# A second engine multiplies the x tiles of a split-precision projection: GpSimd writes the products to scratch, VectorE subtracts

## The chip, the cores and the metric

The kernel runs on one core of a Trainium2 chip. The time is the device time of one execution in microseconds; of the kernel before there are three runs, 1316.72 to 1316.91 us, with a median of 1316.73. Engines are named as in the profile: PE (TensorE), DVE (VectorE), ACT (ScalarE), POOL (GpSimd), SP (SyncE, which issues the loads).

## What is computed

One inference step of a hybrid decoder layer for 256 prompt rows and 8 sample rows (N = 264 columns in the kernel, D = 2048). Only the head of it bears on this case:

```python
xn = rms_norm(x, g_mix)
z = xn @ w_in                       # 2048 x 3584, split among three mixers
...                                 
gates = jax.nn.sigmoid(xn @ w_gate + b_gate)
x = x + (g_a * y_pool + g_b * y_lru + g_c * y_conf) @ w_out
hid = jnp.square(jax.nn.relu(rms_norm(x, g_mlp) @ w_up))
x = x + hid @ w_down
```

Everything is float32, and the result has to be good to nearly that, so the kernel multiplies in three parts (below).

## The kernel before, in words

**Layout.** Channels lie on the 128 partitions, the 264 rows of x along the free dimension. x is 16 tiles of 128x264 (k = 0 to 15). Weights stream from HBM in chunks of two such k-tiles by 512 columns, through six raw slots (`raw`).

**Split products.** TensorE multiplies a rounded format (fp32r). Each operand is therefore kept as a rounded part and a rest: for weights `whi` and `wlo`, for x the two halves of the tile `A`. A product is three matmuls of 128x264: whi by x-high, wlo by x-high, whi by x-low (`mm`, `mm3`, line 255).

**Where each part is made.** For weights, `split` lets ACT cast a chunk to `whi` (L238) and DVE subtract to get `wlo` (L239); for the first four k-tiles, which come in four small head loads with their x tiles, `cast_head` (L248) and `rest_head` (L252) do the same in halves of 256 columns. For x, the tile times the norm's factor of its channel (`gm`, one column for each k, 128 factors) is rounded by `x_high`: on DVE for k = 0 and 1 (L367), on ACT for the others (L369). `x_low` then calls `rest_of` (L171): three DVE instructions of 128x88, each computing x times factor minus the rounded tile and rounding the rest. The normalisation itself is applied later, to the products.

**Order.** The schedule is written out by hand: each engine runs its instructions in the order in which the code issues them, and waits on semaphores. The opening issues for k = 0 to 3: cast of the first half weight, x_high, cast of the second half, x_low, the two weight rests. Then x tiles 4 and 5 and the split of chunk 2; then, in the chunk loop for i = 0 to 4, x tiles 2i+6 and 2i+7 and the split of chunk i+3. PE's matmuls of chunk i follow. For the first four chunks (`by_operand`) they go tile by tile: four with whi and x-high, four with whi and x-low, four with wlo and x-high. From chunk 4 on the three of one output block follow one another.

**Buffers.** `G` is scratch of 24 rows of 128x264. Rows 0 to 7 and 20 to 23 take the squares of x for the norm (L382, L387), later users come after that. POOL has three small memsets at the start, and its next work, the series in `softplus` (L418 and on), at 43 us.

Of the kernel before, what the change touches and what calls it, by code (L numbers as in the profile page):

```python
# [12 lines left out]
ALU = mybir.AluOpType  # L13
# [103 lines left out]
def hybrid_step(ctx: ExitStack, tc: tile.TileContext, first, par_in, st_in, wall, y_out, st_out):  # L117
    nc = tc.nc
# [4 lines left out]
    def f(ap):  # L123
        return ap.bitcast(F32)
# [13 lines left out]
    G = cpool.tile([P, 24, N], F32, name="G")  # L138
# [12 lines left out]
    def both(t, place, row, rows):  # L151
        out = []
        for low in (0, rows * ROW + GAP):
            at = SKEW + row * ROW + place * OCT + low
            out.append(bass.AP(tensor=t.tensor, offset=t[:, at:].offset,
                               ap=[list(t.ap[0]), [HOP, N // (STRETCH * OCT)], [STEP, STRETCH], [1, OCT]]))
        return tuple(out)

    def in_a(k):
        return both(a_all, k // 2, k % 2 + k // 8 * 2, 4)  # L160
# [4 lines left out]
    def v(t):  # L165
        return t.rearrange("p (a b c) -> p a b c", b=STRETCH, c=OCT)

    def rest_of(to, x, g):
        for a in range(N // (STRETCH * OCT)):
            hi, lo, t = to[0][:, a], to[1][:, a], v(x)[:, a]  # L170
            nc.vector.scalar_tensor_tensor(lo, t, g, f(hi), op0=ALU.mult, op1=ALU.subtract)  # L171
# [38 lines left out]
    gm = head[0]  # L210
# [4 lines left out]
    def head_x(k):  # L215
        return head[k // 2][:, head_at(k):head_at(k) + N]
# [145 lines left out]
    def x_of(k):  # L362
        return head_x(k) if k < 4 else X[:, k, :]

    def x_high(k):
        if k < 2:
            nc.vector.tensor_scalar(in_a(k)[0], v(x_of(k)), gm[:, k:k + 1], None, op0=ALU.mult)  # L367
        else:
            nc.scalar.activation(in_a(k)[0], v(x_of(k)), AF.Copy, scale=gm[:, k:k + 1])  # L369

    def x_low(k):
        rest_of(in_a(k), x_of(k), gm[:, k:k + 1])

    def x_tile(k):
        x_high(k)
        x_low(k)
# [588 lines left out]
    for k in range(4):  # L965
        cast_head(k, 0)
        x_high(k)
        cast_head(k, 1)
        x_low(k)
        for h in range(2):  # L970
            rest_head(k, h)
# [220 lines left out]
```

## Time and profile before

| | |
|---|---|
| median of three runs | 1316.73 us (1316.72 to 1316.91) |
| the profiled execution | 1317.18 us |
| its span, first to last instruction | 1315.4 us |
| mean granted TensorE clock | 0.997 |
| first x tile and factors landed | 4.2 us |
| DVE between 4.24 and 25.70 us | 21.39 us busy of 21.46 |
| POOL's first work after the memsets | 43.16 us |

The profiled execution lies 0.45 us above the median, and its span 1.8 us below its own time; the difference is start and end around the instructions. A row of a view by time gives start, length, engine, line, operation, the tile written and the tiles read with their shapes, the count where rows were merged, and in brackets the idle time before it with what ended it. A group's row gives the number, the busy time in us and the mean in ns.

### The profile page before, as it was taken

To read this page: it belongs to the slowest core of one execution; us is meant where nothing else is said; L and a number is where in the kernel's file an instruction comes from. 1 tells how busy PE (TensorE), PEld (TensorE's weight loads), DVE (VectorE), ACT (ScalarE), POOL (GpSimd) and SP (SyncE) were. 2 spreads that over 40 slices of the span, in tenths; PEclk is the share of its full clock that TensorE was granted. 3 is DMA by queue.
4 is the path that set the end of the run, shared out by engine and by line. 5 is a ranking of instruction groups with operands and counts; after the bars stand their busy time and mean duration, and the time that the engine had idled before them with its cause. 6 is when DMAs were issued, how large, how long until landed. Compare 5 with 4: busy or idle time off the path is not lost.

```text
span 1315.4 us, 26547 instructions
## 1 busy us (share of the span) xinstructions
PE 1304.1 (99%) x11421; PEld 1301.1 (99%) x11421; DVE 842.0 (64%) x1130; ACT 720.6 (55%) x1035; POOL 99.5 (8%) x125
## 2 busy tenths in 40 slices
PE   9999999999999999999999999999999999999997
PEld 8999999999999999999999999999999999999996
DVE  8786888776777668666655455655455645465554
ACT  7667677667675645455544334543344533354544
POOL 0230020110102014021000000000000000000012
PEclk9999999999999999999999999999999999999998
DMA  9656556555565555555555555555555555555552
GB/s 331 207 177 234 174 200 213 193 193 193 192 225 193 193 193 191 194 192 193 193 192 192 193 194 193 193 194 192 193 194 194 195 195 194 195 195 195 192 197 76
DMA packets 40822, 257.48 MB, mean 196 GB/s; under 512 B 4481, under 2 KB 6785, under 8 KB 11777
## 3 DMA queue, kind: packets, MB, share of 16 engines
q1 hardware_dynamic: 40272, 255.19, 56.4%
q8 instruction: 89, 1.46, 0.4%
q10 hardware_dynamic: 432, 0.61, 0.1%
q14 instruction: 29, 0.23, 0.1%
HBM read 252.57 MB, written 3.21 MB: 194 GB/s over the span
## 4 chain that ended last, share of the span: by engine, by line
PE 98%; DVE 1%; DMA 0%; issue 0%; DVEq 0%; ACT 0%
PE acc L255 98%; DVE A L171 1%; DMA tmp<-first_dram 0%; DVE y L1078 0%; DVE wlo L239 0%; DVE wlo L252 0%; DVE A L367 0%; DVE acc L1069 0%; DVEq L1169 0%; DVE G L1068 0%; DVE acc L1067 0%; PE acc L1055 0%; PE acc L334 0%; ACT rstd L1062 0%; DVE G L894 0%
## 5 line engine op out<-in xcount | busy, mean ns | idle before, releaser
L239 DVE TENSOR_TENSOR wlo<-raw,whi 128x1024 fp32r<-128x1024 f32 (+1 forms) x478 | 585.2, 1227 | 450.3 <-ACT whi L238 444.5
L238 ACT CAST whi<-raw 128x1024 fp32r<-128x1024 f32 (+1 forms) x478 | 494.5, 1037 | 535.8 <-PE acc L255 490.4
L255 PE MATMUL acc<-A,whi 128*128 128x264 f32 x3968 | 678.0, 275 | 0.3 <-DVE A L367 0.3
L255 PEld LDWEIGHTS acc<-A,whi 128*128 128x128 f32 x3968 | 596.6, 187 | 1.3 <-ACT whi L248 0.8
L255 PE MATMUL acc<-A,wlo 128*128 128x264 f32 x1984 | 541.3, 275 | 0.6 <-DVE wlo L239 0.4
L255 PEld LDWEIGHTS acc<-A,wlo 128*128 128x128 f32 x1984 | 370.2, 187 | 1.4 <-DVE wlo L239 1.4
L255 PE MATMUL acc<-xn,whi 128*128 128x264 f32 x2048 | 349.9, 275 | 0.0
L255 PEld LDWEIGHTS acc<-xn,whi 128*128 128x128 f32 x2048 | 308.5, 188 | 0.0
L255 PE MATMUL acc<-xn,wlo 128*128 128x264 f32 x1024 | 281.0, 274 | 0.0
L255 PEld LDWEIGHTS acc<-xn,wlo 128*128 128x128 f32 x1024 | 192.0, 188 | 0.0
L255 PE MATMUL acc<-Q,whi 128*128 128x264 f32 x776 | 144.9, 275 | 0.0
L255 PE MATMUL acc<-LH,whi 128*128 128x264 f32 x768 | 143.7, 276 | 0.0
L255 PEld LDWEIGHTS acc<-Q,whi 128*128 128x128 f32 x776 | 122.4, 188 | 0.0
L255 PEld LDWEIGHTS acc<-LH,whi 128*128 128x128 f32 x768 | 121.2, 188 | 0.0
L255 PE MATMUL acc<-Q,wlo 128*128 128x264 f32 x388 | 106.6, 275 | 0.0
L255 PE MATMUL acc<-LH,wlo 128*128 128x264 f32 x384 | 105.7, 275 | 0.0
L864 POOL TENSOR_TENSOR G<-G 128x264 f32<-128x264 f32 x28 | 25.7, 919 | 754.0 <-ACT G L862 753.0
L255 PEld LDWEIGHTS acc<-Q,wlo 128*128 128x128 f32 x388 | 72.8, 188 | 0.0
L255 PEld LDWEIGHTS acc<-LH,wlo 128*128 128x128 f32 x384 | 72.0, 188 | 0.0
L648 ACT ACTIVATE G<-tmp,par 128x256 f32<-128x256 f32 x120 | 54.3, 499 | 2.5 <-DVE G L651 1.7
L651 DVE TENSOR_TENSOR G<-G 128x1024 f32<-128x1024 f32 x30 | 38.2, 1274 | 0.0
L897 DVE TENSOR_TENSOR X<-X,acc 128x264 f32<-128x264 f32 x79 | 28.7, 423 | 6.5 <-PE acc L255 6.5
(173 smaller groups left out, 522.1 us busy)
## 6 DMA issues: line engine op xcount, KB each, us to landing
raw<-wall_dram SPq DMA_DIRECT2D x226, 1024.0 KB, 4.8
raw<-wall_dram SPq DMA_DIRECT2D x12, 512.0 KB, 5.1
raw<-first_dram SPq DMA_DIRECT2D x6, 512.0 KB, 7.9
X<-first_dram SPq DMA_DIRECT2D x6, 264.0 KB, 7.8
raw<-wall_dram SPq DMA_DIRECT2D x5, 256.0 KB, 2.9
tmp<-first_dram SPq DMA_DIRECT2D x3, 388.0 KB, 4.5
y_dram<-y SPq DMA_DIRECT2D x3, 264.0 KB, 2.2
tmp<-st_dram SPq DMA_DIRECT2D x4, 188.0 KB, 5.1
```

What stands on the lines that cost most here:

```text
L171: nc.vector.scalar_tensor_tensor(lo, t, g, f(hi), op0=ALU.mult, op1=ALU.subtract)
L238: nc.scalar.copy(h, r)
L239: nc.vector.tensor_tensor(lo, r, f(h), op=ALU.subtract)
L255: nc.tensor.matmul(ps[:, :N], w[k == 1], x[k == 2], start=start, stop=stop)
L648: nc.scalar.activation(dst[:, ct, :TP], vext[:, ct, k:k + TP], AF.Copy, scale=par[:, w:w + 1])
L651: nc.vector.tensor_tensor(VC[:, :, :TP], VC[:, :, :TP], src[:, :, :TP], op=ALU.add)
L864: nc.gpsimd.tensor_tensor(sq2, sq2, t, op=ALU.add)
L897: nc.vector.tensor_tensor(X[:, m, :], X[:, m, :], ps[:, :N], op=ALU.add)
```

## The change

GpSimd now multiplies each x tile by its factors, in float32, and leaves the product in a scratch row, `G[:, 8 + k % 12, :]`. `x_low` is one subtraction on DVE over the whole tile: scratch row minus rounded tile, rounded. And the rounded tile for k = 1 is made by GpSimd instead of DVE. ACT's rounded tiles for k from 2 on stay as they were.

```diff
     def x_high(k):
         if k < 2:
-            nc.vector.tensor_scalar(in_a(k)[0], v(x_of(k)), gm[:, k:k + 1], None, op0=ALU.mult)
+            eng = nc.gpsimd if k else nc.vector
+            eng.tensor_scalar(in_a(k)[0], v(x_of(k)), gm[:, k:k + 1], None, op0=ALU.mult)
         else:
             nc.scalar.activation(in_a(k)[0], v(x_of(k)), AF.Copy, scale=gm[:, k:k + 1])
+        t = G[:, 8 + k % 12, :]
+        nc.gpsimd.tensor_scalar(t, x_of(k), gm[:, k:k + 1], None, op0=ALU.mult)
 
     def x_low(k):
-        rest_of(in_a(k), x_of(k), gm[:, k:k + 1])
+        hi, lo = in_a(k)
+        nc.vector.tensor_tensor(lo, v(G[:, 8 + k % 12, :]), f(hi), op=ALU.subtract)
```

How it stands on DVE in the opening, from the first x tile on (with - what stood there before, with + what stands there now; `tmp_70` and `tmp_71` are the two tiles of the head loads with x, factors and weights for k = 0, 1 and k = 2, 3):

```order
-L367 TENSOR_SCALAR A<-tmp_70 128x3x11x8
-L171 SCALAR_TENSOR_TENSOR A<-tmp_70,A 128x11x8 x3
+L368 TENSOR_SCALAR A<-tmp_70 128x3x11x8
+L376 TENSOR_TENSOR A<-G,A 128x3x11x8
 L252 TENSOR_TENSOR wlo<-tmp_70,whi 128x256 x2
-L367 TENSOR_SCALAR A<-tmp_70 128x3x11x8
-L171 SCALAR_TENSOR_TENSOR A<-tmp_70,A 128x11x8 x3
+L376 TENSOR_TENSOR A<-G,A 128x3x11x8
 L252 TENSOR_TENSOR wlo<-tmp_70,whi 128x256 x2
-L171 SCALAR_TENSOR_TENSOR A<-tmp_71,tmp_70,A 128x11x8 x3
+L376 TENSOR_TENSOR A<-G,A 128x3x11x8
```

Three pieces became one instruction, which reads a row of `G` and so waits for POOL; the second TENSOR_SCALAR is gone from DVE. The weight rests between them stay where they were.

POOL's list at the same place, before (its three memsets, then the start of `softplus`):

```order
L358 MEMSET qtmp 128x4x15
L418 ISA
L418 TENSOR_TENSOR G<-G 128x8
L419 TENSOR_TENSOR G<-G 128x8
L421 MEMSET G 128x8
```

and now:

```order
L358 MEMSET qtmp 128x4x15
L372 ISA
L372 TENSOR_SCALAR G<-tmp_70 128x264
L368 TENSOR_SCALAR A<-tmp_70 128x3x11x8
L372 TENSOR_SCALAR G<-tmp_70 128x264
L372 TENSOR_SCALAR G<-tmp_71,tmp_70 128x264 x2
L372 TENSOR_SCALAR G<-X,tmp_70 128x264 x12
L422 TENSOR_TENSOR G<-G 128x8
```

Seventeen instructions came in ahead of `softplus`: the product for k = 0, the rounded tile for k = 1 and then its product, and the products of the other tiles, each as soon as its x has landed (and, from k = 12 on, as soon as DVE has read the scratch row that it reuses). The ISA row, which stands ahead of POOL's first operation on tensors, moved from `softplus` to the first product.

## The prediction

> **What bounds the kernel now.** I read the page first: the busy shares and the chain that ended last.
>
> ```profile
> PE 1304.1 (99%) x11421; PEld 1301.1 (99%) x11421; DVE 842.0 (64%) x1130; ACT 720.6 (55%) x1035; POOL 99.5 (8%) x125
> PE 98%; DVE 1%; DMA 0%; issue 0%; DVEq 0%; ACT 0%
> ```
>
> TensorE (PE) is busy for 99% of the span and holds 98% of the chain. The change touches the opening alone, where x is split into a rounded tile and its rest, so the next view is the chain of waits of the first 80 us.
>
> ```profile
> 19.62 1.15 DVE wlo L239
> 20.77 0.04 issue
> 20.82 22.01 PE acc L255 x191
> ...
> 42.95 37.06 PE acc L255 x326
> ```
>
> Up to 20.82 us the chain runs through DVE (and the first landing); from there it is PE without a break. So the opening is worth what PE loses before 20.82 us, and no more. That is counted from the busy time by window, for the matmuls of L255 (columns: window, its length, PE busy and count, weight loads, clock, DMA share, GB/s), and named in the waits of the weight loads between 4 and 21 us.
>
> ```profile
> 4.87:20.82 15.95, 15.37 (x122) 14.24 (x122) 1.00 1.03 397
> 20.82:42.83 22.01, 22.01 (x192) 21.96 (x193) 1.00 0.75 260
> ...
> PEld acc L255 <- DVE wlo L239: 1.2, 3, 0.6
> PEld acc L255 <- ACT whi L248: 0.8, 1, 0.8
> PEld acc L255 <- DVE A L171: 0.4, 2, 0.2
> ```
>
> After 20.82 us a matmul costs 22.01 / 192 = 0.1146 us. The 122 of the opening would take 13.98 us at that rate, and took 15.95: **1.97 us are lost**, all but the first 0.8 us of ACT wait (which lies before the first matmul) on DVE. That is the most that the change can give: 0.15% of 1317 us. My bound between a change and no change is 0.2% (2.63 us), about what a measurement of this kernel can tell from no change. So a gain that counts is out of reach from the start; the question is how much of the 1.97 us comes back, or whether something is paid on top.
>
> DVE has no hole in that stretch (columns as above, with DVE, ACT, POOL behind the weight loads):
>
> ```profile
> 4.24:25.70 21.46, 20.56 (x165) 19.15 (x164) 21.39 (x68) 19.09 (x36) 0.00 (x0) 1.00 1.01 384
> ```
>
> 21.39 of 21.46 us are DVE work and POOL does nothing. PE's last wait on it, for the second weight rest `wlo` of chunk 5, ends at 20.82 us; each microsecond that DVE reaches this instruction sooner or later goes to PE, until another wait takes over.
>
> **What goes from DVE.** In order of time, one x tile of DVE's list, and further on the same subtraction as the new one (128x264, two SBUF operands, rounded output):
>
> ```profile
> 6.10 0.48 DVE L367 TENSOR_SCALAR A<-tmp 128x264 fp32r<-128x264 f32 x1
> 6.62 0.75 DVE L171 SCALAR_TENSOR_TENSOR A<-tmp,A 128x88 fp32r<-128x88 f32 x3
> 7.29 0.76 DVE L252 TENSOR_TENSOR wlo<-tmp,whi 128x256 fp32r<-128x256 f32 x2
> ...
> 98.75 1.80 DVE L517 TENSOR_TENSOR L<-G,L 128x264 fp32r<-128x264 f32 x5
> 100.46 1.22 DVE L239 TENSOR_TENSOR wlo<-raw,whi 128x1024 fp32r<-128x1024 f32 x1
> ```
>
> Instructions overlap a little, so I count from start to start. Three L171 pieces: 7.29 - 6.62 = 0.67 us. One L517: (100.46 - 98.75) / 5 = 0.34 us. Each x tile saves 0.33 us. The second rounded tile (L367) goes to POOL and saves 6.62 - 6.10 = 0.52 us. Up to the `wlo` of chunk 5 DVE handles 12 x tiles: 12 x 0.33 + 0.52 = **4.5 us less** of its own work.
>
> **What POOL adds.** Seventeen instructions of 128x264: 16 products into scratch and one rounded tile. POOL idles, but not for free, as the one place shows where POOL and DVE both work on SBUF in small pieces:
>
> ```profile
> 83.35 1.65 DVE L488 TENSOR_TENSOR G<-G,tmp 128x1024 f32<-128x1024 f32 x1
> 84.92 1.23 DVE L239 TENSOR_TENSOR wlo<-raw,whi 128x1024 fp32r<-128x1024 f32 x1
> 86.08 1.25 DVE L488 TENSOR_TENSOR G<-G,tmp 128x1024 f32<-128x1024 f32 x1
> 87.25 1.21 DVE L239 TENSOR_TENSOR wlo<-raw,whi 128x1024 fp32r<-128x1024 f32 x1
> ...
> 83.87 1.20 POOL L505 COPY st<-tmp 128x24 f32<-128x24 f32 x1
> 85.01 1.24 POOL L750 COPY st<-qtmp 128x60 f32<-128x60 f32 x1
> ```
>
> A COPY of 24 elements takes 1.20 us: it stands until DVE's L488 is over (83.35 + 1.65 = 85.00) and ends 0.07 us later. The COPY of 60 ends at 86.25, 0.10 us after DVE's L239 (86.15). So the two engines take turns, one whole instruction each, where DVE reads two SBUF operands. And DVE waits in its turn: behind the COPY of 60 its instruction takes 1.25 instead of 1.21 us. How it looks with a POOL instruction of the new length, but with two operands:
>
> ```profile
> 252.31 1.77 DVE L651 TENSOR_TENSOR G<-G 128x1024 f32<-128x1024 f32 x1
> ...
> 249.83 4.85 POOL L817 TENSOR_TENSOR tmp<-G 128x264 f32<-128x264 f32 x4 [69.04 <-DVE G L814]
> ```
>
> DVE takes 1.77 us for what takes 1.21 alone: 0.56 us. The new subtractions and all the `wlo` instructions read two operands from SBUF, so nearly every POOL instruction falls between two of them.
>
> **The price of one POOL instruction to DVE is the unknown of this sum.** The trace has no TENSOR_SCALAR of POOL longer than 8 elements.
>
> ```profile
> 46.71 1.22 DVE L464 TENSOR_TENSOR tmp<-G,rstd 128x1024 f32<-128x1024 f32 x1
> 46.94 1.05 POOL L424 TENSOR_SCALAR G<-G 128x8 f32<-128x8 f32 x1
> 48.07 0.20 POOL L423 TENSOR_TENSOR G<-G 128x8 f32<-128x8 f32 x1
> ```
>
> It ends at 47.99, 0.06 us after DVE's 47.93: as a COPY of that length would. From below: the two COPYs differ by 36 elements and 0.03 us, 0.8 ns an element; 264 elements cost DVE 0.04 + 204 x 0.0008 = 0.20 us. From above: the two-operand 0.56 us. The new instruction has one tensor operand, so it is nearer to the COPY, with a factor for each partition to fetch on top and one strided output: I take **0.25 us**. Where DVE would have waited anyway it could cost less, down to nothing, but DVE has no holes now.
>
> The Trainium skill, GPSIMD Engine Reference, section 3.1, gives a one-input loop about 1.03 cycles an element at 1.2 GHz. By that 264 elements last 0.23 us, an estimate beside the COPY's 0.21, and the sum below would be some 0.2 us under the 0.25 case's.
>
> By the `wlo` of chunk 5, POOL has run the rounded tile and the products of tiles 0 to 13: 15 instructions (the scratch holds 12 rows, so it may run ahead of DVE, as far as x has landed). ACT's list shows that x of tiles 12 and 13 is there by 16.91:
>
> ```profile
> 16.91 0.92 ACT L369 ACTIVATE A<-X,tmp 128x264 fp32r<-128x264 f32 x2
> ```
>
> **Sum.** DVE at its `wlo` of chunk 5: -4.5 + 15 x 0.25 = **-0.75 us**. With 0.20 it is -1.5, with 0.56 it is +3.9; it turns at 0.30 us an instruction. PE follows DVE there, as it waits at that point now. The smaller waits before (0.4 us on L171, wlo of chunk 2) shorten with it and hand the time on to the later wait; they are not added again. Behind it nothing else moves: from 20.82 us on PE is the chain. What else could hide or give: ACT casts `whi` as before (19.09 of 21.46 us busy), and its next wait is on landings; SP's loads behind chunk 7 are released by DVE's split and move with it; POOL's next own work starts at 43 us. A chance that x1's rounded tile comes late: it queues on POOL behind the product of tile 0, and PE wants it when tile 0 is done, at 6.1 us at the earliest; x1 lands by 5.18,
>
> ```profile
> 5.18 0.71 ACT L248 CAST whi<-tmp 128x256 fp32r<-128x256 f32 x2 [0.23 <-DMA tmp<-first_dram]
> ```
>
> plus one DVE turn (0.42) and its own 0.4: 6.0, before DVE's 6.58 of now. The product of tile 1 stands behind it and makes the first rest late by a turn, which is in the 15.
>
> The profiled execution took 1317.18 us (span 1315.4), 0.45 above the median of 1316.73. With -0.75 it comes to 1316.4, and on the scale of the median to **1316.0 us**.
>
> **Rivals.** *More relief:* an instruction of POOL costs 0.20 or less, since some of them fall on instructions that read PSUM or on new holes: -1.5 to the whole -1.97, 1314.8 to 1315.2.
>
> *The turns cost more than the rest saved (other side):* the mechanism is the alternation on the opening's DVE list, the price 0.56 us as with two operands. For: every POOL row in the trace beside a two-operand DVE row shows it. Against: one operand, and the COPY's slope. It gives +3.9, 1320.6; slower than before from 0.30 on, by more than 0.2% from (4.5 + 2.63) / 15 = 0.48 us on.
>
> *POOL starts late:* ahead of POOL's first product the order has an ISA row, which before stands ahead of L418, with 42 us to spare until POOL's next work. If its effect takes until a time T, DVE's first subtraction, which stands ahead of everything else in its list, waits until T + 0.44 (0.40 for the product, 0.04 for the signal) instead of starting at 4.76; the rows bound T only by x0's landing at 4.2 and by 43. I price it at 3 us behind the landing: T = 7.2, 2.9 us late, less the 0.75: +2.1, 1318.8; slower by over 0.2% from T = 7.7 on. Against it: the DMA queues of the first 12 us hold next to nothing of the instruction kind.
>
> ```profile
> q14 instruction: 1, 0.00, 0.0%
> ```
>
> The Trainium skill, GPSIMD Engine Reference, section 2.1, says that the first call of a freshly loaded kernel pays about 6 us for the load, without a visible instruction. By that T would be near 7, an estimate, and the time 1318.7; no row here shows such a load.
>
> **How the numbers follow.** Forecast, -2.0 to 0 with its likeliest at -0.75, more relief included: 0.45. Price between 0.30 and 0.48, or POOL a few microseconds late: 0 to +2.63: 0.28. Price of two operands: 0.12, and POOL later than 7.7 us: 0.13, both above +2.63. Faster by over 0.2%: 0.02, as only 1.97 us are there. So faster 0.02, same 0.73, slower 0.25. The range runs from the whole relief (1314.8) to the two-operand price (1320.6), and leaves out a POOL that is both late and dear, or very late.
>
> **What would show it.** DVE rows of the new L376 at 0.43 us alone, up to 0.6 behind POOL: price confirmed; near 0.9: the two-operand price. POOL's first product at 4.2 us, and not at 7 or later. PE's last wait in the chain near 20.1 instead of 20.8 us. I am wrong if PE's matmuls before chunk 5 lose more than 1.97 us, or if the span moves by more than PE's losses do.

## The result, and the profile after

| | before | change |
|---|---|---|
| median of 17 runs each, same chip | 1316.90 us (1316.72 to 1317.28) | 1319.33 us (1319.02 to 1319.64) |
| ratio, 95% interval | | 1.0018 (1.0011 to 1.0025) |
| the profiled execution and its span | 1317.18, 1315.4 us | 1319.33, 1317.5 us |
| x of tile 0 landed, in the profile | 4.22 us | 3.92 us |
| TensorE's last wait of the opening ends | 20.82 us | 21.70 us |
| last matmul to the last semaphore | 9.59 us | 10.31 us |

The change costs 2.43 us (0.18%; 1.4 to 3.3 us by the interval). The forecast was a gain of 0.75. A time is the median of a kernel's executions; one execution of experiment 11, at 4845.82 us, is the only one that lies far from the others of its kernel. TensorE is still the bound (the page, after: busy time and instructions of each engine):

```profile
PE 1304.8 (99%) x11421; PEld 1301.6 (99%) x11421; DVE 839.4 (64%) x1097; ACT 720.5 (55%) x1035; POOL 121.1 (9%) x142
```

It now loses more ahead of 20.82 us. The same window as in the prediction shows 14.64 us of matmuls where 15.37 stood before, 116 in place of 122.

```profile
4.87:20.82 15.95, 14.64 (x116) 13.74 (x116) 1.00 1.02 394
```

The waits between 4 and 26 us (engine, line, what it waited for, us in total, times, longest) tell what TensorE waited for; the first row is what DVE itself now waits for:

```profile
DVE A L376 <- POOL G L372: 4.3, 8, 0.8
PEld acc L255 <- DVE wlo L239: 1.7, 3, 0.8
PE acc L255 <- DVE wlo L239: 0.9, 2, 0.6
```

DVE, which had no hole here before, waits 4.3 us for POOL's products. POOL's list by time shows why:

```profile
3.99 0.95 POOL L372 TENSOR_SCALAR G<-tmp 128x264 f32<-128x264 f32 x1 [2.92 <-DMA tmp<-first_dram]
4.93 1.21 POOL L368 TENSOR_SCALAR A<-tmp 128x264 fp32r<-128x264 f32 x1
6.12 0.98 POOL L372 TENSOR_SCALAR G<-tmp 128x264 f32<-128x264 f32 x1
...
9.50 16.11 POOL L372 TENSOR_SCALAR G<-X,tmp 128x264 f32<-128x264 f32 x12
```

From 3.99 to 25.6 us there is no hole in it: seventeen instructions end to end. None waits for x to land after the first, and POOL is never more than one tile ahead of DVE. A product takes 0.95 us where it need not wait for DVE and 16.11 / 12 = 1.34 us on the mean of the last twelve. The same, seen from DVE's list (the bracket is the idle time before the row; the row by itself is the `wlo` of chunk 5 in the kernel before):

```profile
19.55 1.22 DVE L239 TENSOR_TENSOR wlo<-raw,whi 128x1024 fp32r<-128x1024 f32 x1
```
```profile
7.13 0.43 DVE L376 TENSOR_TENSOR A<-G,A 128x264 fp32r<-128x264 f32 x1 [0.84 <-POOL G L372]
11.99 0.43 DVE L376 TENSOR_TENSOR A<-G,A 128x264 fp32r<-128x264 f32 x1 [0.76 <-POOL G L372]
17.25 0.43 DVE L376 TENSOR_TENSOR A<-G,A 128x264 fp32r<-128x264 f32 x1 [0.21 <-POOL G L372]
17.60 1.51 DVE L239 TENSOR_TENSOR wlo<-raw,whi 128x512 fp32r<-128x512 f32 x2
19.03 0.63 DVE L376 TENSOR_TENSOR A<-G,A 128x264 fp32r<-128x264 f32 x1
20.22 1.43 DVE L239 TENSOR_TENSOR wlo<-raw,whi 128x1024 fp32r<-128x1024 f32 x1
```

The last row, the `wlo` of chunk 5, is the one on which the prediction's sum was made; before it started at 19.55 by the same view (the chain gives 19.62, since it counts a row only from the end of the one before). Three rows of the change in which DVE stands behind a product (0.63 for 0.43, 1.43 for 1.21, and 1.51 for 1.28 on the pair) put the turn, which is what DVE loses to one POOL instruction, at 0.2 us. The groups between 4 and 26 us, before and after, say the same of the means:

```profile
L239 DVE TENSOR_TENSOR wlo<-raw,whi 128x512 fp32r<-128x512 f32 x6 | 3.9, 683 | 0.0
L252 DVE TENSOR_TENSOR wlo<-tmp,whi 128x256 fp32r<-128x256 f32 x8 | 3.0, 421 | 0.0
```
```profile
L376 DVE TENSOR_TENSOR A<-G,A 128x264 fp32r<-128x264 f32 x16 | 7.4, 466 | 4.3 <-POOL G L372 4.3
L239 DVE TENSOR_TENSOR wlo<-raw,whi 128x512 fp32r<-128x512 f32 x6 | 4.5, 794 | 0.0
L252 DVE TENSOR_TENSOR wlo<-tmp,whi 128x256 fp32r<-128x256 f32 x8 | 3.8, 516 | 0.0
```

Half of the instructions meet a turn: 516 - 421 = 95 ns on the mean, 0.19 each for four of eight.

**The ledger of DVE up to the `wlo` of chunk 5.** Its own work is 4.5 us less, as forecast. Ten rows stand behind a turn: 10 x 0.205 = 2.05. Six waits for POOL: 0.57, 0.84, 0.76 and three of 0.21, together 2.80; and as instructions otherwise overlap by 0.08 us (0.42 long, 0.34 from start to start), each wait costs that too, 0.48. Sum: -4.5 + 2.05 + 2.80 + 0.48 = +0.83. Measured: 20.22 - 19.55 = 0.67 later, with x landed 0.30 earlier, so 0.97; the ledger leaves 0.14 us open.

**Where the 2.15 us between the two spans lie**, by the start of the same matmul (by its number in order) in both traces:

| at, before | TensorE later by | what it waits for there |
|---|---|---|
| 20.82 us | 0.88 | DVE, `wlo` of chunk 5 |
| 23.78 us | 1.03 | DVE, `wlo` of chunk 6 |
| 83.94 us | 1.21 | DVE, `wlo` |
| 101.74 us | 1.43 | DVE, `wlo`, behind other DVE work |
| last matmul | 1.43 | |
| end of the span | 2.15 | the stores of y |

So less than half of the loss is in the place the prediction looked at (from equal landings, 1.20 of 2.46 us, experiment 11). The chain, after (start, us, what), shows the part near 102 us too:

```profile
20.22 1.44 DVE wlo L239
...
21.70 22.14 PE acc L255 x191
...
101.98 1.15 DVE wlo L239
...
103.17 6.91 PE acc L255 x58
```

Ahead of 20.22 this view goes by way of weight loads and ACT, although ACT's cast of chunk 5 was over at 17.14 and DVE's own row before the `wlo` had waited for POOL; in experiments 4 and 11 the chain there is POOL's list.

And the last 0.72 us lie behind the last matmul. The transfers between 1300 and 1320 us (the queue's kind, packets, MB, share; and of an issue: KB, us to landing), before and after:

```profile
y_dram<-y SPq DMA_DIRECT2D x1, 330.0 KB, 3.0
```
```profile
q14 instruction: 1, 0.01, 0.2%
y_dram<-y SPq DMA_DIRECT2D x1, 330.0 KB, 3.7
```

In the list of packets this one is of 8192 bytes, takes 608 ns, starts 7.18 us before the end and is followed by a store's packet of 311 ns (109 at most for the others of its size in this stretch). Before, the last packet of instructions starts 19.7 us ahead of the end.

### The profile page after: what moved, and what is told of

It reads as the page before. It is cut to its first block, busy times and chain, and to the rows that moved or that the text cites. A ratio compares the mean times of both kernels' runs of the same rounds, so it can differ in the third digit from the quotient of the medians.

```text
span 1317.5 us, 26538 instructions
## 1 busy us (share of the span) xinstructions
PE 1304.8 (99%) x11421; PEld 1301.6 (99%) x11421; DVE 839.4 (64%) x1097; ACT 720.5 (55%) x1035; POOL 121.1 (9%) x142
## 4 chain that ended last, share of the span: by engine, by line
PE 97%; DMA 1%; DVE 1%; ACT 0%; SPq 0%; issue 0%; DVEq 0%; ACTq 0%
PE acc L255 97%; DMA raw<-first_dram 1%; DVE y L1082 0%; DVE wlo L239 0%; SPq L224 0%; ACT whi L238 0%; DVE L L521 0%; DVE tmp L602 0%; ACT A L370 0%; DVE acc L1073 0%; DVEq L1173 0%; DVE G L1072 0%; DVE acc L1071 0%; PE acc L1059 0%; PE acc L334 0%
## 5 line engine op out<-in xcount | busy, mean ns | idle before, releaser
L239 DVE TENSOR_TENSOR wlo<-raw,whi 128x1024 fp32r<-128x1024 f32 (+1 forms) x478 | 586.3, 1230 | 450.5 <-ACT whi L238 444.8
L255 PE MATMUL acc<-A,whi 128*128 128x264 f32 x3968 | 678.2, 275 | 0.4 <-DVE A L376 0.3
L255 PEld LDWEIGHTS acc<-A,whi 128*128 128x128 f32 x3968 | 596.5, 187 | 1.2 <-DVE A L376 0.8
L255 PE MATMUL acc<-A,wlo 128*128 128x264 f32 x1984 | 541.2, 275 | 1.3 <-DVE wlo L239 1.1
L255 PEld LDWEIGHTS acc<-A,wlo 128*128 128x128 f32 x1984 | 370.1, 187 | 2.4 <-DVE wlo L239 2.1
L255 PE MATMUL acc<-xn,whi 128*128 128x264 f32 x2048 | 349.9, 275 | 0.0
L255 PEld LDWEIGHTS acc<-xn,whi 128*128 128x128 f32 x2048 | 308.3, 187 | 0.0
L255 PE MATMUL acc<-xn,wlo 128*128 128x264 f32 x1024 | 280.7, 274 | 0.0
L255 PEld LDWEIGHTS acc<-xn,wlo 128*128 128x128 f32 x1024 | 191.8, 187 | 0.0
L255 PE MATMUL acc<-Q,whi 128*128 128x264 f32 x776 | 144.9, 275 | 0.0
L255 PE MATMUL acc<-LH,whi 128*128 128x264 f32 x768 | 143.7, 275 | 0.0
L255 PEld LDWEIGHTS acc<-Q,whi 128*128 128x128 f32 x776 | 122.4, 187 | 0.0
L255 PEld LDWEIGHTS acc<-LH,whi 128*128 128x128 f32 x768 | 121.1, 187 | 0.0
L255 PE MATMUL acc<-Q,wlo 128*128 128x264 f32 x388 | 106.5, 274 | 0.0
L255 PE MATMUL acc<-LH,wlo 128*128 128x264 f32 x384 | 105.5, 275 | 0.0
L255 PEld LDWEIGHTS acc<-Q,wlo 128*128 128x128 f32 x388 | 72.7, 187 | 0.0
L255 PEld LDWEIGHTS acc<-LH,wlo 128*128 128x128 f32 x384 | 72.0, 187 | 0.0
```

What stands on the lines that cost most here:

```text
L239: nc.vector.tensor_tensor(lo, r, f(h), op=ALU.subtract)
L255: nc.tensor.matmul(ps[:, :N], w[k == 1], x[k == 2], start=start, stop=stop)
```

## The experiments

Two theories at the start: **W**, DVE waits for POOL's own list, which is the bound; **T**, the turns cost more than was reckoned. The times of the first four stand beside the kernel before at 1317.07 us, the next four at 1317.01, the last four at 1317.04. A ratio stands with its 95% interval. The edits of experiments 1, 3, 4, 7 and 11 start from the change, those of 2, 5, 6, 9, 10 and 12 from the kernel before.

**1. The products, but not used.**

```diff
     def x_low(k):
-        hi, lo = in_a(k)
-        nc.vector.tensor_tensor(lo, v(G[:, 8 + k % 12, :]), f(hi), op=ALU.subtract)
+        rest_of(in_a(k), x_of(k), gm[:, k:k + 1])
```

> GpSimd makes all its products and the rounded tile for k = 1, but x_low is that of the kernel before, so no one waits for a product. Theory W (the change is late because VectorE waits for GpSimd's own list, some 1.25 us a product): what is left is the turns, some 13 lengthenings of 0.2 us to the wlo of chunk 5, less 0.5 for the rounded tile: +2 us over the kernel before, 1318.5 to 1319.5, and no VectorE wait on a product. Theory T (the turns on the shared path to SBUF are what costs, more than 0.3 us each): +3.5 or more, 1320.5 and above.

1320.12 us, 1.0024 (1.0015 to 1.0034): +3.05, between the two. POOL's turns alone, in the chain and in the group of the old subtraction:

```profile
22.98 3.14 PE acc L255 x25
```
```profile
L171 DVE SCALAR_TENSOR_TENSOR A<-X,tmp,A 128x88 fp32r<-128x88 f32 x31 | 9.0, 353 | 0.0
```

TensorE's wait ends 2.16 us later than before, with one wait on POOL of 0.8 us (the rounded tile) and nothing saved but 0.52. The pieces take 353 ns where they took 301. So 16 products nobody reads cost about 3 x 0.052 = 0.16 us each; that is no more than the prediction had. The 0.33 us that the new subtraction saves a tile is more, which speaks against T as an explanation of the loss; W's own number for this run was too low, as it left the old subtractions' turns out.

**2. No products.** The subtraction takes x itself (the factor is left out of the rest), and both rounded tiles are DVE's.

```diff
     def x_low(k):
-        rest_of(in_a(k), x_of(k), gm[:, k:k + 1])
+        hi, lo = in_a(k)
+        nc.vector.tensor_tensor(lo, v(x_of(k)), f(hi), op=ALU.subtract)
```

> No product at all: x_low is the one subtraction, of the unscaled x tile (so the rest lacks the factor), and both rounded tiles of k = 0, 1 are on VectorE as before. Both theories: VectorE's saving alone, 4 us to the wlo of chunk 5, of which PE can use at most 1.97: 1314.9 to 1315.4. If the single subtraction itself is dearer than 0.34 us beside the other work, the time stays near 1316.9.

1316.28 us, 0.9995 (0.9986 to 1.0004): -0.8, with no change inside its interval. This is the change with its products for nothing (the second rounded tile, 0.52 us, stays with DVE), and it does not give the 1.97 us either. TensorE is 1.37 us earlier at the `wlo` of chunk 5; 1.1 behind 84 us and 0.87 behind 101 us, and there it stays, as the span shows too (1314.5 for 1315.4). DVE has a new wait between 4 and 26 us:

```profile
DVE wlo L239 <- ACT whi L238: 1.9, 3, 0.8
```

ACT's casts are next in line, as its 19.09 us of work in 21.46 might have told. Without products the idea gives 0.8 us here.

**3. A constant for the factor.** The product is x times 1.0 in place of the column of factors; length, row and wait are the same.

```diff
-        nc.gpsimd.tensor_scalar(t, x_of(k), gm[:, k:k + 1], None, op0=ALU.mult)
+        nc.gpsimd.tensor_scalar(t, x_of(k), 1.0, None, op0=ALU.mult)
```

> The products with the constant 1.0 in place of the factor of each partition (so the scratch row holds x unscaled); all else as in the change. If fetching the factors is what makes a product 0.95 us, it falls to 0.4 to 0.5 us alone, GpSimd runs ahead and theory W gives 1315.5 to 1316.5. If the length of the operation is in its 264 elements, a product stays at 0.9 us or more and the time at 1319.3. Theory T has no change from the shorter instruction unless the turns get shorter too.

1318.00 us, 1.0008 (0.9999 to 1.0017): +0.93, where the change has +2.43. POOL's list by time:

```profile
9.18 9.62 POOL L372 TENSOR_SCALAR G<-X 128x264 f32<-128x264 f32 x10
19.99 2.33 POOL L372 TENSOR_SCALAR G<-X 128x264 f32<-128x264 f32 x2 [1.19 <-DMA X<-first_dram]
```

A product takes 0.96 in place of 1.34 us on the mean and still 0.87 alone, so that neither case of the expectation came as written (it had 0.4 to 0.5, or 0.9 and more). Yet now POOL does what the prediction had assumed: it runs ahead of DVE until it waits for x to land. DVE's turns stayed (L252 at 517 ns, L239 of 512 at 822), its waits fell from 4.3 to 1.5 us, all in the first tiles, and TensorE is 0.13 us late at the `wlo` of chunk 5 in place of 0.88. So the length of a product is what counts: W. Beside DVE the column of factors makes up a good quarter of that length; what the remaining 0.87 us consist of was not tried. At its last matmul TensorE is only 0.18 us late; 0.56 us of the time lie behind it (see experiments 9 and 10).

**4. The second rounded tile back on DVE.**

```diff
-            eng = nc.gpsimd if k else nc.vector
-            eng.tensor_scalar(in_a(k)[0], v(x_of(k)), gm[:, k:k + 1], None, op0=ALU.mult)
+            nc.vector.tensor_scalar(in_a(k)[0], v(x_of(k)), gm[:, k:k + 1], None, op0=ALU.mult)
```

> The change with the rounded tile for k = 1 back on VectorE. Theory W: GpSimd's list is 1.2 us shorter from the second tile on, VectorE's 0.5 longer: the wait for the product of k = 1 falls by about 0.8, the wlo of chunk 5 comes up to 1.2 us earlier: 1318.0 to 1318.6. Theory T: VectorE gains a turn (0.2) and pays 0.5: 1319.4 to 1319.8.

1319.20 us, 1.0016 (1.0008 to 1.0025): +2.13, near the change's +2.43. Neither theory's number was met in full. The chain says what happened: with an instruction less, POOL waits for the landing of tile 2 and from there its list is the chain.

```profile
1.64 5.26 DMA tmp<-first_dram
...
6.99 9.54 POOL G L371 x8
...
17.32 1.16 POOL G L371
...
18.52 1.45 POOL G L371
```

W as to the mechanism; the 1.2 us that I took off POOL's list came off ahead of a landing.

**5. Products for odd tiles from 5 on alone.**

```diff
+    POOL_K = range(5, 16, 2)
...
+        if k in POOL_K:
+            nc.gpsimd.tensor_scalar(G[:, 8 + k % 12, :], x_of(k), gm[:, k:k + 1], None, op0=ALU.mult)
...
-        rest_of(in_a(k), x_of(k), gm[:, k:k + 1])
+        if k not in POOL_K:
+            rest_of(in_a(k), x_of(k), gm[:, k:k + 1])
+            return
+        hi, lo = in_a(k)
+        nc.vector.tensor_tensor(lo, v(G[:, 8 + k % 12, :]), f(hi), op=ALU.subtract)
```

> GpSimd makes the products of tiles 5, 7, 9, 11, 13 and 15 alone; the other ten tiles take their rest in three pieces on VectorE as before, and both rounded tiles of k = 0 and 1 are VectorE's again. Theory W (VectorE waits for GpSimd's list, at 1.25 us a product): with every second tile GpSimd has some 2.75 us for each of its products and VectorE waits on it less than 0.2 us in all; up to the weight rest of chunk 5 five tiles save 5 x 0.33 = 1.65 us and six turns cost 6 x 0.2 = 1.2 us, so the time is 0.2 to 0.6 us under the kernel before, and PE's last wait of the opening ends 0.3 to 0.5 us earlier. Theory T (turns cost over 0.3 us each): 6 x 0.35 = 2.1 us against 1.65, the time is 0.3 to 0.6 us over the kernel before.

1317.05 us, 1.0000 (0.9991 to 1.0009); span 1315.0. DVE no longer waits for POOL at all, and TensorE's last wait ends at 20.39:

```profile
20.39 5.62 PE acc L255 x47
```

0.43 us earlier than in the first profile of before, 0.17 than in the second (below): as W has it. The execution times show no gain (1317.05 beside 1317.01), and W's 0.2 to 0.6 is missed there. The spans do show one: 1314.8 us on the median of the executions for 1315.2 before, so that the 0.4 us are lost outside the span. All eleven executions last 2.20 to 2.27 us longer than their spans, those of every other kernel here 1.73 to 1.86, and the trace has an 8 KB packet of instructions 0.97 us behind the last instruction; whether that packet is the cause was not tried. T's +0.3 to +0.6 is not there.

**6. Products from tile 4 on.** The same edit with `POOL_K = range(4, 16)`.

> GpSimd makes the products from tile 4 on; tiles 0 to 3 take their rest on VectorE as before, and the rounded tiles of k = 0 and 1 too. Theory W: GpSimd's list now begins at the landing of tile 4 (about 9 us) with no early tiles queued ahead; its products still follow at about 1.25 us each, 2.5 us a chunk, while VectorE and PE take 2.75 us a chunk, so after the first one or two VectorE's waits on it are below 0.5 us in all. Up to the weight rest of chunk 5 eight tiles save 2.6 us and ten turns cost 2.0: the time is 0 to 0.6 us under the kernel before. Theory T (0.35 us a turn): 3.5 us against 2.6, 0.9 us over the kernel before. If instead VectorE still waits over 1 us on GpSimd's rows, a product's length in turns has been taken too small, and the time comes out 0.5 to 1.2 us over.

1318.44 us, 1.0011 (1.0002 to 1.0020): +1.43. A miss for W's main number; its other case came, with DVE's waits over 1 us and a time a little over its 0.5 to 1.2 (TensorE is 0.93 us late at its last matmul). POOL's list by time, and DVE's waits between 4 and 26 us:

```profile
8.72 16.36 POOL L373 TENSOR_SCALAR G<-X,tmp 128x264 f32<-128x264 f32 x12 [7.65 <-DMA X<-first_dram]
```
```profile
DVE A L380 <- POOL G L373: 2.4, 6, 0.8
```

Again no hole. The reason is in the pace of the alternation: by the single instructions of this trace a product lasts 1.22 us beside a subtraction of 0.43, 1.45 beside a `wlo` of 0.69 and 1.70 when one of 1.21 us stands ahead. The pair of a chunk thus takes POOL 1.22 + 1.45 = 2.67, later 1.22 + 1.70 = 2.92 us. The DVE list that it was to relieve took 2 x 0.67 + 1.20 = 2.54 and then 2 x 0.67 + 1.14 = 2.48 us a chunk before. POOL's share alone is slower than all of DVE's old list, at whichever tile it starts.

**7. One product for two tiles**, from tile 4 on, with the factors as a second operand.

```diff
-        nc.gpsimd.tensor_scalar(t, x_of(k), gm[:, k:k + 1], None, op0=ALU.mult)
+        if k < 4:
+            nc.gpsimd.tensor_scalar(G[:, 8 + k % 12, :], x_of(k), gm[:, k:k + 1], None, op0=ALU.mult)
+        elif k % 2 == 0:
+            r = 8 + k % 12
+            nc.gpsimd.tensor_tensor(G[:, r:r + 2, :], X[:, k:k + 2, :],
+                                    gm[:, k:k + 2, None].to_broadcast([P, 2, N]), op=ALU.mult)
```

> From tile 4 on GpSimd makes one product for two tiles, as a two-operand instruction of 128x528 with the factor as a broadcast second operand, so there are six turns in place of twelve. Theory W: what counts is when a product ends; an instruction of 528 elements with two operands takes 1.5 to 2.2 us and the first tile of each pair waits for the second tile's landing as well; VectorE's waits on GpSimd go from 2.8 us up to the weight rest of chunk 5 to 3 to 5 us, and the time is 0.5 to 2 us over the change's. Theory T: the number of turns counts, each 0.2 to 0.35 us whatever its length; six fewer take 1.2 to 2 us off, and the time is at the kernel before's or up to 0.5 us over it. If a turn's price goes with its length and operands instead, VectorE's rows behind GpSimd rise by 0.8 to 1.2 us rather than by 0.2.

1320.89 us, 1.0030 (1.0018 to 1.0041): +3.88, the slowest. POOL is twice as fast a tile and waits for landings between; the price has gone over to DVE:

```profile
12.91 1.09 POOL L375 TENSOR_TENSOR G<-X,tmp 128x528 f32<-128x528 f32 x1 [0.79 <-DMA X<-first_dram]
```
```profile
9.90 1.30 DVE L380 TENSOR_TENSOR A<-G,A 128x264 fp32r<-128x264 f32 x1
```

1.30 - 0.42 = 0.88 us a turn, 0.44 for each tile, in place of 0.2. So six long turns are no cheaper than twelve short ones: the third case of the expectation. Length and number of operands were changed together, so which of them sets the price is open. T, by which the number of turns counts, falls here. W's number for the time was met (+1.45 over the change), but not by its waits: DVE no longer waits for the products of the pairs.

**8. The kernel before once more.**

> The kernel before once more, for a second profile of it. Theory W takes PE's last wait of the opening as a property of the program: it ends at 20.8 us, give or take 0.3 with x's landing at 4.2 us. If the small waits of PE near 84 and 102 us (0.2 us each in every kernel with the change or a part of it) show here too, they are run to run variation and not the change's.

1316.91 us, span 1315.1. TensorE's last wait of the opening ends at 20.56, and all later matmuls come 0.25 us ahead of those of the first profile: no step at 84 or 102 us, which therefore belong to the change; 9.60 us from the last matmul to the end.

Now the two parts outside the opening. **9. and 10. More POOL instructions in the kernel before**: 17, as many as the change adds, and 41.

```diff
+    pad = cpool.tile([P, 4], F32, name="pad")
...
         if m == KD - 1:
+            for _ in range(17):
+                nc.gpsimd.memset(pad, 0.0)
             later(4, lambda: total_fold(pk, G[:, 10, :], sq2))
```

> The kernel before with 17 more GpSimd instructions (memsets of four elements in a tile of their own), placed near 615 us, where GpSimd has nothing to do and TensorE sets the time. The opening is untouched. Theory F (a fetch of 8 KB of GpSimd's instructions, which stands in the list of DMA packets of queue 14, comes at a fixed place of its instruction list; 17 more instructions bring it among the stores of y, one of which then lands 0.7 us later): the last semaphore comes 10.1 to 10.3 us behind TensorE's last matmul instead of 9.6, a packet of queue 14 stands 6 to 8 us before the end, and the time is 0.4 to 0.8 us over the kernel before with TensorE as early as there. Rival (the late stores of the change come from the opening or are chance): 9.6 us and no difference.

> The kernel before with 41 such memsets in place of 17, as a control. Theory F: the fetch has come before the stores begin; 9.6 us behind the last matmul and no difference to the kernel before (within 0.2 us). If the memsets themselves cost time: at least what 17 of them cost, 0.4 us or more over.

With 17: 1317.58 us, 1.0004 (0.9995 to 1.0013), span 1315.9 against 1315.4 and 1315.1; 10.13 us from the last matmul to the end. With 41: 1317.08, 1.0000 (0.9992 to 1.0009), span 1315.1, 9.59 us. The transfers between 1300 and 1320 us with 17:

```profile
q14 instruction: 1, 0.01, 0.1%
y_dram<-y SPq DMA_DIRECT2D x1, 330.0 KB, 3.5
```

The fetch stands among the stores with 17 and not with 41, so it is the place of the fetch in POOL's list that counts and not the number of instructions. It starts 4.5 us before the end, later than I had said. The same packet stands 4.5 to 7.0 us before the end in experiments 1, 3 and 4, and their ends come 10.11 to 10.15 us behind the last matmul; in the kernel before and in experiments 2, 8, 10, 11 and 12 no such packet stands there, and it is 9.58 to 9.60. That the packet itself holds up the store is read from this, not shown apart. The runs' +0.54 us agrees with the 0.53 us of the trace, though by their interval alone they could not tell it from zero.

**11. The change with 24 such memsets.**

> The change with 24 more memsets of that kind, at the same place. Theory F: the fetch comes before the stores begin, the last semaphore 9.6 us behind the last matmul instead of 10.3, and the time is 0.5 to 0.8 us under the change's (1318.5 to 1318.9), with the opening as in the change (TensorE's last wait at 21.7). Rival: as the change, 1319.2 to 1319.5.

1318.93 us, 1.0013 (1.0004 to 1.0022): +1.89, so 0.54 less than the change's +2.43, within the expected 0.5 to 0.8 (by the bare times 0.40); 9.60 us from the last matmul to the end. In this profile x landed at 4.23 us, as in before's, and the chain of the opening is POOL's list nearly from end to end (its line numbers are one higher):

```profile
4.32 0.95 POOL G L373
5.27 1.20 POOL A L369
6.47 10.53 POOL G L373 x9
...
17.51 2.65 POOL G L373 x2
...
20.54 1.44 DVE wlo L240
...
22.02 22.14 PE acc L256 x191
```

TensorE's wait ends 1.20 us later than before, the last matmul starts at 1307.54 and so 1.74 later. 1.74 + 0.72 = 2.46 us is the change from equal landings, and the runs gave 2.43.

**12. DVE late behind the opening.**

```diff
+        if i == 5:
+            nc.vector.tensor_tensor(G[:, 8:12, :], X[:, 8:12, :], X[:, 12:16, :], op=ALU.add)
         for half in (0, 1) if i < 2 else (None,):
             split(i + AHEAD, half)
```

> The kernel before with one more VectorE instruction of 128x1056 (an addition of x tiles into rows of scratch that nothing reads), behind the weight rest of chunk 7, near 27 us: VectorE is late by about 1.17 us from there, and not before. Theory L (VectorE's list from 25 to 102 us has no slack, so that its lateness at 25 us is handed to TensorE at 84 and 102 us): TensorE's last wait of the opening stays at 20.6 to 20.9 us, TensorE is late by 0.9 to 1.2 us behind 102 us, and the time is 0.9 to 1.2 us over the kernel before. Rival (from 20.8 us on TensorE alone is the chain, as the prediction had it): no difference.

1318.14 us, 1.0008 (0.9999 to 1.0017): +1.10. The chain:

```profile
20.70 22.00 PE acc L255 x191
...
82.75 1.66 DVE wlo L239
84.46 12.42 PE acc L255 x107
...
101.52 1.15 DVE wlo L239
102.71 7.37 PE acc L255 x62
```

TensorE leaves the opening on time (0.12 us early), is 0.75 us late at 84 us and 0.97 at 102: what DVE loses at 27 us TensorE pays then. On the way to 84 us the lateness passes through ACT, whose L485 waits for DVE's L488 and stands ahead of the cast that this `wlo` needs.

## Why the prediction was wrong, step by step

- **The step that failed:** "the scratch holds 12 rows, so it may run ahead of DVE, as far as x has landed", with "0.40 for the product". A product takes 0.95 us alone and 1.22 to 1.70 in alternation with DVE, and sixteen of them and a tile fill POOL from 3.99 to 25.6 us without a hole. No rival made POOL's own list the bound; the price to DVE had been bounded from both sides, the duration on POOL from none, although rows that the prediction shows had it: beside DVE's work, 4.85 / 4 = 1.21 us for POOL's L817 of 128x264 and 1.05 us for L424 of only 8 elements. Experiments 3, 4, 6 and 11 show it: shorter products take the waits away (3), a later start of the list does not (6), and the chain runs along POOL's list (4 and 11).
- **The price of a turn** was right, 0.205 us for 0.25, and there were ten up to the `wlo` of chunk 5 and not fifteen: POOL had finished 13 instructions by then, and three of them lengthened no row of DVE's. By itself that would have been -4.5 + 2.05 = -2.45, better than the forecast; the waits, 3.28 with the lost overlap, turn it to +0.83.
- **The saving of 4.5 us** of DVE's own work was right: the ledger closes within 0.14 us with it.
- **The ceiling of 1.97 us** was above what the idea can give; without any products it is 0.8, as ACT's casts come next and 0.5 us of TensorE's lead in the opening is lost again by 101 us (experiment 2).
- **"Behind it nothing else moves: from 20.82 us on PE is the chain"** fell. The chain showed TensorE alone from there on, but DVE had next to no slack behind it. The trace of before has a wait that tells so: between 75 and 110 us, near 102, `PEld acc L255 <- DVE wlo L239: 0.2, 1, 0.2`. Up to the end of the 16 tiles DVE is 1.52 us late (the `wlo` that started at 25.61 starts at 27.12), still 1.45 at 44 us and 1.43 at 100 us, and TensorE, 1.03 late, comes to the same 1.43 by 102 us: 0.40 us more. Experiment 12 shows that lateness of DVE alone does this.
- **The end** was in no step: 0.72 us, which come and go with the place of an instruction fetch among the stores (experiments 9, 10 and 11).
- **x1's rounded tile** ended at 6.14 us, for 6.0 forecast. What came late was the product behind it (7.10), for which DVE waited 0.84 us.
- **POOL starts late** did not happen: its first product starts 0.07 us after x has landed. The Trainium skill, GPSIMD Engine Reference, section 2.1, speaks of some 6 us for a load at a kernel's first call; no run here shows it.
- **The price of two operands** did not apply to the change. Experiment 7 has a price of that kind, 0.88 us, for two operands and 528 elements.
- **Both signs of being wrong** came: from its first matmul in the change, at 4.56, to the end of its last wait TensorE loses 21.70 - 4.56 - 13.98 = 3.16 us in place of 1.97, and the span moves by 2.15 us, more than that loss does. The signs for the price (0.43 alone, up to 0.6 behind POOL) and for POOL's prompt start came as forecast too.
- The time lies in the range, and in the case "0 to +2.63" that the prediction held for a dearer turn or a late start. Neither was the cause, so that the range held by luck.

By the rate in the Trainium skill, GPSIMD Engine Reference, section 3.1, the loop over 264 elements comes to 0.23 us, an estimate. That is near the 0.2 us that DVE loses to a product; it is a quarter of the 0.95 that the product lasts. The Trainium skill, SBUF — State Buffer, "Who interferes with whom", says that whoever issues first gets the shared pair of ports for the whole instruction and the other is fully blocked; here DVE loses 0.2 us to an instruction of 0.95 to 1.7, and the measurement decides.

## What to carry to other kernels

When work goes to a slower engine, sum up that engine's list before anything else: the duration of one piece beside the other engine's work, times the number of pieces, against the time in which the relieved engine did all of its old work. What the neighbour loses is the second question. An engine off the chain needs its slack measured as far as the next place where the chain's engine waits for it: a chain that is all TensorE from 20.82 us on says nothing of how close the next wait was. And on the scale of 0.1% the end of the program counts: added instructions can move a fetch in among the last stores.

## What was not expected of the hardware

- A POOL product of 264 elements with a factor from a column takes 0.95 us alone, 0.87 with a constant; beside DVE's two-operand work 1.22 to 1.70, with the constant 0.96 on the mean (0.86 to 1.44).
- A product ends about 0.73 us after the DVE instruction for which it stood back (in experiment 6: 18.59 to 19.32, 19.79 to 20.52, 21.47 to 22.20 us).
- DVE loses 0.2 us to it (0.16 where DVE works in pieces of 88 elements), though it lasts five times as long, and 0.88 us to one that reads two operands of 528 elements.
- With one 8 KB fetch of instructions, 0.3 to 0.6 us long, among the stores of y, the program ends 0.52 to 0.72 us later (five traces). The Trainium skill, Runtime: NRT & Kernel Launch, "Instruction fetch mechanics", calls the cost of a fetch mostly hidden; at this place it is not. What makes experiments 6 and 7, where the fetch starts 0.04 and 0.08 us behind the last instruction, end 0.36 and 0.44 us later than before behind their last matmul was not tried.
